# Splitting the first load of a Poisson loss kernel: row 0 of log_input in 16 KB runs, rows 1 to 3 behind it in 48 KB runs

## Chip, cores, metric

One core of one Trainium2 chip. The metric is the device time of one execution in microseconds (us), median over repeated runs; lower is better.

Engines: DVE is VectorE, ACT is ScalarE, SP is the sequencer that issues the loads (SPq in the profile), DMA the core's sixteen transfer engines. x stands for log_input, t for target.

## The reference

```python
batch, dim = 1024, 4096          # log_input and target, float32
loss = np.exp(log_input) - target * log_input
return np.mean(loss, axis=-1)    # 1024 results
```

Two inputs of 16.8 MB are read once, 4 KB are written. Each partition holds 8 neighbouring rows of 4096 elements (16 KB each), so several rows of one partition are one contiguous run in memory.

## The kernel before

All loads are issued by SP on one queue, in this order, each with its own semaphore:

```python
TAIL = [("x", 24), ("t", 12), ("t", 12), ("x", 6), ("t", 5), ("x", 2), ("t", 3)]  # 32nds of row 7
...
    loads = []
    for first, rows in ((0, 4), (4, 2), (6, 1)):
        loads += [("x", first * d, rows * d), ("t", first * d, rows * d)]
    # then TAIL, the pieces of row 7
...
    for i, (what, lo, w) in enumerate(loads):
        if what == "x" and lo in (6 * d, 7 * d):     # rows 6 and 7 reuse the buffer of rows 0 to 3
            free = 1 if lo == 6 * d else 4
            nc.sync.wait_ge(exp_done, free)
            nc.sync.wait_ge(prod_done, free)
        src = x_v if what == "x" else t_v
        dma = nc.sync.dma_start(out=place(what, lo, w), in_=src[:, lo : lo + w])
        dma.then_inc(landed[i] if i < len(loads) - 1 else last_ready, 16)
        if lo < 6 * d:
            early.append(dma.ins)
    before_first_barrier(nc, early)                  # issued ahead of everything else
```

ACT takes exp of one row at a time with the row's sum; DVE multiplies one row of t by the row of x, also with the sum; ACT joins both sums of a row:

```python
    for k, (lo, w, i) in enumerate(x_work):          # ACT, a row at a time
        row, col = lo // d, lo % d
        if col == 0 and row >= 2:
            join(row - 2, k)                         # waits for DVE's product of row - 2
        elif col == 0 and row == 1:
            nc.scalar.wait_ge(exp_done, k)
        nc.scalar.activation(... Exp ...).wait_op(landed[i], 16, "sem-ge")...
        # cut
    for j, (lo, w, i) in enumerate(t_work):          # DVE, a row at a time
        x_load = next(ix for a, wx, ix in x_work if a + wx >= lo + w)
        if j == 0 or x_load > t_work[j - 1][2]:
            nc.vector.wait_ge(landed[x_load], 16)
        nc.vector.tensor_tensor_reduce(... t = t * x, sum ...).wait_op(landed[i], 16, "sem-ge")...
```

The last DVE instruction waits for everything, adds up row 7 and releases the store.

## Time and profile before

| | before |
|---|---|
| time | 84.06 us, 3 runs, 84.04 to 84.06 |
| span of the profiled execution | 82.9 us |
| DVE, ACT busy | 43%, 40% |
| DMA queue | 2016 packets, 95.5% of sixteen engines' time |
| x rows 0 to 3 landed, t rows 0 to 3 landed | 22.10 us, 41.44 us |

The lines of the page and of the timeline are in the prediction below. Two terms it uses: a *packet* is one run of one partition; each of the sixteen engines moves eight partitions of every load, so every load is eight data packets per engine, whatever the length of the runs (the trace has 256 packets of 64 KB for the first two loads). A load has *landed* when the last of the sixteen engines has reported its part.

What ACT and DVE waited for before (columns: total us, times, longest us):

```profile
DVE t_big L175 <- DMA t_big<-in_target_dram: 43.6, 3, 41.4
ACT e_dump L155 <- DMA x_big<-in_log_input_dram: 24.0, 4, 17.8
ACT join_dump L141 <- DVE parts L175: 20.4, 6, 16.3
ACT L155 <- PEq L48: 3.0, 1, 3.0
```

The last line is the wait at the program's first barrier. ACT's two large waits stand one behind the other: 17.8 us for its first row and then 16.3 us for DVE's first product.

### The profile page before, as it was taken

The numbers are of one execution on the slowest core, as the hardware profiler recorded it, in microseconds if no ns is written. First come the engines' busy times: TensorE is split into PE (matmuls) and PEld (weight loads), VectorE is DVE, ScalarE is ACT, GpSimd is POOL, SyncE is SP. The second block draws the span as 40 slices with busy tenths as digits, with TensorE's granted clock in tenths as the row PEclk, the third lists the DMA queues.
The fourth block names the chain that finished last, engine by engine and source line by source line (L and its number), as shares of the span: only waits on it lengthen the run. The fifth ranks groups of instructions, "written<-read, shape, count | busy, mean of one in ns | idle before, by whom it ended". The sixth has DMA issues, their size and how long they took to land.

```text
span 82.9 us, 131 instructions
## 1 busy us (share of the span) xinstructions
DVE 35.6 (43%) x22; ACT 33.2 (40%) x35; POOL 0.3 (0%) x5
## 2 busy tenths in 40 slices
DVE  0000000000000000000099999999469996994992
ACT  0500000000399920000000897979793496019460
POOL 0000000000000000000000000000000000000000
DMA  9199999929999992999699799899899999999950
GB/s 506 63 443 506 506 506 506 443 127 443 506 506 506 506 443 127 443 506 506 269 490 474 316 474 490 380 411 490 364 403 435 443 435 393 433 397 421 393 184 2
DMA packets 2016, 33.56 MB, mean 405 GB/s; under 512 B 352, under 2 KB 608, under 8 KB 1120
## 3 DMA queue, kind: packets, MB, share of 16 engines
q1 hardware_dynamic: 2016, 33.56, 95.5%
HBM read 33.55 MB, written 0.00 MB: 405 GB/s over the span
## 4 chain that ended last, share of the span: by engine, by line
DMA 72%; DVE 18%; issue 4%; SPq 3%; ACT 1%
DMA t_big<-in_target_dram 49%; DMA x_big<-in_log_input_dram 23%; DVE t_big L175 17%; SPq L129 3%; DVE t_big L193 1%; ACT e_dump L155 1%; DVE parts L175 0%; SPq L127 0%; DVE all_loss L193 0%
## 5 line engine op out<-in xcount | busy, mean ns | idle before, releaser
L175 DVE CUSTOM_DVE_ANT_0 t_big<-t_big,x_big 128x4096 f32<-128x4096 f32 (+2 forms) x8 | 26.2, 3306 | 43.8 <-DMA t_big<-in_target_dram 43.6
L155 ACT ACTIVATE e_dump<-x_big 128x4096 f32<-128x4096 f32 (+3 forms) x8 | 21.8, 2730 | 24.2 <-DMA x_big<-in_log_input_dram 24.0
L175 DVE CUSTOM_DVE_ANT_0 t_mid<-t_mid,x_mid 128x4096 f32<-128x4096 f32 x2 | 8.8, 4424 | 2.0 <-DMA t_mid<-in_target_dram 2.0
L141 ACT ACTIVATE join_dump<-parts 128x2 f32<-128x2 f32 x7 | 1.4, 203 | 20.4 <-DVE parts L175 20.4
L155 ACT ACTIVATE e_dump<-x_mid 128x4096 f32<-128x4096 f32 x2 | 7.1, 3568 | 0.0
L155 ACT ACT_TABLE_LOAD x1 | 1.3, 1283 | 3.0 <-PEq L48 3.0
L155 ACT ACTIVATION_READ_ACCUMULATOR e_dump<-x_big 128x1 f32 x8 | 1.5, 186 | 0.0
L141 ACT ACTIVATION_READ_ACCUMULATOR join_dump<-parts 128x1 f32 x7 | 1.3, 186 | 0.0
L193 DVE CUSTOM_DVE_ANT_0 t_big<-t_big,x_big 128x390 f32<-128x390 f32 x1 | 0.6, 566 | 0.1
L175 DVE DVE_READ_ACCUMULATOR2_ANT parts<- 128x1 f32 x7 | 0.6, 81 | 0.0
L155 ACT ACTIVATION_READ_ACCUMULATOR e_dump<-x_mid 128x1 f32 x2 | 0.4, 186 | 0.0
L175 DVE DVE_READ_ACCUMULATOR2_ANT t_big<- 128x1 f32 x3 | 0.2, 83 | 0.0
L136 POOL MEMSET x_big<- 128x6 f32 x1 | 0.1, 103 | 2.5 <-POOLq L48 2.5
L227 POOL MEMSET const-bfloat16-1.0<- 128x1 bf16 x1 | 0.1, 101 | 0.0
L227 POOL MEMSET const-uint8-127<- 128x1 uint8 x1 | 0.1, 101 | 0.0
L227 POOL MEMSET const-float32-0.0<- 128x1 f32 x1 | 0.1, 98 | 0.2 <-issue 0.2
L227 POOL MEMSET const-float32-1.0<- 128x1 f32 x1 | 0.1, 98 | 0.0
L193 DVE DVE_READ_ACCUMULATOR2_ANT all_loss<- 128x1 f32 x1 | 0.1, 84 | 0.0
## 6 DMA issues: line engine op xcount, KB each, us to landing
x_mid<-in_log_input_dram SPq DMA_DIRECT2D x1, 4096.0 KB, 50.2
t_mid<-in_target_dram SPq DMA_DIRECT2D x1, 4096.0 KB, 59.5
x_big<-in_log_input_dram SPq DMA_DIRECT2D x1, 2048.0 KB, 19.8
t_big<-in_target_dram SPq DMA_DIRECT2D x1, 2048.0 KB, 24.3
x_big<-in_log_input_dram SPq DMA_DIRECT2D x1, 1536.0 KB, 15.3
t_big<-in_target_dram SPq DMA_DIRECT2D x2, 768.0 KB, 17.6
x_big<-in_log_input_dram SPq DMA_DIRECT2D x1, 384.0 KB, 18.8
t_big<-in_target_dram SPq DMA_DIRECT2D x1, 320.0 KB, 19.1
```

The costliest lines, as they stand in the source:

```text
L129: dma = nc.sync.dma_start(out=place(what, lo, w), in_=src[:, lo : lo + w])
L136: nc.gpsimd.memset(big["x"][:, 4 * d : 4 * d + n_parts], -1.0).then_inc(ones_done, 1)
L141: nc.scalar.activation(out=join_dump[:, 2 * row : 2 * row + 2], in_=parts[:, 2 * row : 2 * row + 2], func=ACT_F.Copy, scale=inv_d, accum_o ...
L155: nc.scalar.activation(out=e_dump[:, col : col + w], in_=place("x", lo, w), func=ACT_F.Exp, bias=0.0, scale=1.0, accum_out=parts[:, 2 * ro ...
L175: nc.vector.tensor_tensor_reduce(out=place("t", lo, w), in0=place("t", lo, w), in1=place("x", lo, w), scale=-1.0, scalar=0.0, op0=ALU.mult ...
L193: nc.vector.tensor_tensor_reduce(out=place("t", lo, w + n_parts), in0=place("t", lo, w + n_parts), in1=place("x", lo, w + n_parts), scale= ...
L227: nc = _bacc.Bacc("TRN2", target_bir_lowering=False, num_devices=1)
```

## The change

The intent, as far as the diff shows it: let exp of row 0 begin as soon as row 0 is there, instead of when all four rows are. DVE's bookkeeping is changed so that it waits once for each load of x.

```diff
     loads = []
-    for first, rows in ((0, 4), (4, 2), (6, 1)):
+    loads += [("x", 0, d), ("x", d, 3 * d), ("t", 0, 4 * d)]
+    for first, rows in ((4, 2), (6, 1)):
         loads += [("x", first * d, rows * d), ("t", first * d, rows * d)]
...
+    waited = set()
     for j, (lo, w, i) in enumerate(t_work):
...
-        if j == 0 or x_load > t_work[j - 1][2]:
+        if x_load not in waited:
             nc.vector.wait_ge(landed[x_load], 16)
+            waited.add(x_load)
```

## The prediction

> **What bounds the kernel now.** I read the page first. Each compute engine is busy under half of the span, while the DMA row is full almost to the end and the one queue takes 95.5% of the sixteen engines' time:
>
> ```profile
> span 82.9 us, 131 instructions
> DVE 35.6 (43%) x22; ACT 33.2 (40%) x35; POOL 0.3 (0%) x5
> ...
> DVE  0000000000000000000099999999469996994992
> ACT  0500000000399920000000897979793496019460
> ...
> DMA  9199999929999992999699799899899999999950
> ...
> q1 hardware_dynamic: 2016, 33.56, 95.5%
> ...
> DMA 72%; DVE 18%; issue 4%; SPq 3%; ACT 1%
> ```
>
> The two empty-looking slices in the DMA row's first half are not idleness: a 64 KB packet takes 2.418 us and a slice is 2.07 us, so now and then a slice is credited with no finished packet. I checked this in the packet records: chained end to start, the sixteen engines run from 1.0 us to about 80 us with no gap over 0.12 us (the output store apart). The "DVE 18%" of the chain of waits is a detour: from 41.4 to 58.9 us the chain goes through DVE only because the last loads are issued once DVE has freed their buffer, but these loads then wait behind others in the queue. Next, the timeline shows when each load landed (what the idle time in brackets ended on) and when each issue was made:
>
> ```profile
> 0.00 0.38 SPq L129 DMA_DIRECT2D x_big<-in_log_input_dram  x1
> 0.43 0.42 SPq L129 DMA_DIRECT2D t_big<-in_target_dram  x1
> 0.89 0.43 SPq L129 DMA_DIRECT2D x_mid<-in_log_input_dram  x1
> 1.37 0.55 SPq L129 DMA_DIRECT2D t_mid<-in_target_dram  x1
> ...
> 22.10 3.59 ACT L155 ACTIVATE e_dump<-x_big 128x4096 f32<-128x4096 f32 x1 [17.84 <-DMA x_big<-in_log_input_dram]
> ...
> 41.44 4.42 DVE L175 CUSTOM_DVE_ANT_0 t_big<-t_big,x_big 128x4096 f32<-128x4096 f32 x1 [41.44 <-DMA t_big<-in_target_dram]
> ...
> 45.91 0.20 ACT L141 ACTIVATE join_dump<-parts 128x2 f32<-128x2 f32 x1 [16.29 <-DVE parts L175]
> 45.96 0.33 SPq L129 DMA_DIRECT2D x_big<-in_log_input_dram  x1
> ...
> 59.00 0.33 SPq L129 DMA_DIRECT2D x_big<-in_log_input_dram  x1
> ...
> 60.87 4.43 DVE L175 CUSTOM_DVE_ANT_0 t_mid<-t_mid,x_mid 128x4096 f32<-128x4096 f32 x1 [1.96 <-DMA t_mid<-in_target_dram]
> ...
> 70.65 4.42 DVE L175 CUSTOM_DVE_ANT_0 t_big<-t_big,x_big 128x4096 f32<-128x4096 f32 x1 [1.00 <-DMA t_big<-in_target_dram]
> ...
> 80.30 0.39 ACT L155 ACTIVATE e_dump<-x_big 128x256 f32<-128x256 f32 x1 [0.23 <-DMA x_big<-in_log_input_dram]
> ```
>
> To see here: ACT starts at 22.10 when all four rows of log_input (8.4 MB) are there, DVE at 41.44 when four rows of target are. The loads of row 6 are issued at 45.96, when x_mid and t_mid are still in transit (t_mid lands at 60.87), so the queue has about 15 us of work in hand. The last row's loads are issued from 59.00, with everything up to the 70.65 landing still in the queue: some 11.6 us in hand. So no refill ever finds the queue empty. The end is the stream's own end (last log_input piece at 80.28), then one short exp, the last DVE instruction, and the store. The time is therefore: when the stream starts, plus what 33.5 MB take, plus a tail of about 2.6 us that the change does not touch.
>
> **What the Trainium skill says.**
> - "DMA: Bandwidth & Descriptors", section "Where 436 GB/s comes from": 16 ports of 32 bytes at 850 MHz give a ceiling of 435.2 GB/s. The trace agrees: a 64 KB packet in 2.418 us is 27.1 GB/s on an engine, times 16 is 434 GB/s. There is nothing left to win from larger runs.
> - The same page, section "Why small descriptors are slow (HBM only)": each packet carries a fixed overhead of a few cycles. The trace agrees in kind: the records' median packets are 2.418 us (64 KB), 1.213 (32 KB), 0.611 (16 KB). Twice 1.213 less 2.418 is 8 ns per packet, and four times 0.611 less 2.418 over three is 9 ns.
> - The same page, section "Queues, rings and completion order": each engine consumes descriptors in ring order. The trace agrees: the loads land in the order of issue, so a load split in two keeps the place of its bytes in the stream.
> - The same page, "Latency and other measured facts", row "HBM row pitch at large powers of two": copies lose rate at partition pitches of 512 KiB and up. The pitch here is 8 rows of 16 KB, 128 KB, before and after. Row 6 already travels in 16 KB runs at that pitch, at the full 0.611 us (longest 0.636), so this case's trace shows no loss.
>
> **The change part by part.**
> Removed: one issue of 128 runs of 64 KB, that is 8 packets per engine. Added: one issue of 128 x 16 KB, one of 128 x 48 KB, together 16 packets per engine; one more completion write per engine (9 ns in the records); one more issue on SP; one more semaphore wait on DVE. The bytes stay the same.
>
> 1. Stream. From the landings, a row of either input takes (41.44 - 22.10)/4 = 4.835 us in 64 KB runs and (70.65 - 60.87)/2 = 4.89 us in 16 KB runs. The 16 KB row has 8 packets per engine, the 64 KB one 2 per row: 0.055 us for 6 packets, 9 ns each, the same as from the records. Eight more packets per engine are 8 x 9 = 0.07 us, and with the completion write about 0.08 us. All of it is on the path, because the stream has no slack anywhere.
>
> 2. SP. A fifth early issue takes about 0.45 us (the others: 0.38 to 0.55). SP then reaches the first barrier later, and what stands at 2.97 us for ACT (its table load, 1.28 us) moves to about 3.4, done by 4.7. Row 0 arrives later than that (next point), so it is hidden. The first issue is still first, and the second follows while the first has 4.9 us of packets to move, so no engine runs dry: 0.
>
> 3. ACT. Start-up, completion and queueing before the first landing are 22.10 - 4 x 4.835 = 2.76 us. Row 0 lands at 2.76 + 4.89 = 7.65 and exp starts there, 14.45 us earlier; rows 1 to 3 land at about 22.2. Then exp of row 1 runs from 22.2 to 25.9. Exp of row 2 stands behind the join of row 0, which needs DVE's product of row 0, which needs target at 41.5. So ACT stops at 25.9 and not 29.6, and both orders meet again at 45.9. The 14.45 us turn wholly into a longer wait: 0 on the path.
>
> 4. DVE. It begins with target's landing, about 41.52. The new wait between rows 0 and 1 is on data that landed 20 us ago; as an estimate from the 17 ns that the trace gives to SP's own semaphore waits and the 70 ns by which two products overlap now (45.79 against the former's end at 45.86), it costs up to 0.1 us. DVE has 1.96 us of slack before t_mid: 0. The wait that frees the last row's buffer moves from 58.94 to about 59.1, against 11.6 us of queue in hand: 0.
>
> Sum: 84.06 + 0.08 + 0 + 0 + 0 = 84.14 us, say 84.1.
>
> **The rivals.**
> - The earlier exp shortens the program (the change's likely intent). For it: ACT idles 17.84 us and begins 14 us earlier after the change. Against it: ACT's next wait is 16.29 us for DVE's product, and DVE waits 41.44 us for target, which comes behind all of log_input's four rows still. For a gain, target's bytes would have to move forward; they don't. This rival would give some 80 us or less; I give it 1 in 100.
> - The start of the stream changes. The first packet of each engine took 2.76 to 3.63 us against 2.418 later, so 0.3 to 1.2 us go there, and the engine with 3.63 keeps some 0.3 us of lag to the end of the early loads, where it sets the landings. If the excess is one latency per engine, short first packets pay it just the same and nothing moves. If short packets even out the laggard, up to 0.3 us are won (83.8); if each of the first few short packets pays some of it, 0.3 to 0.5 us are lost (84.5). This, and not the packet overhead, sets the width of my range.
> - Shorter runs lower the rate of HBM, or the queue holds too few entries. For it: twice the packets. Against it: row 6's 16 KB packets at full rate, and up to ten loads in the queue after 59.00 with issues of 0.33 to 0.45 us each, none held up. A loss of 5% on the first 8.4 MB would be 1 us (85.1); 2% of the whole time would need 1.7 us.
>
> **Range and chances.** The centre is 84.1. The runs before differ by 0.02 us, so the width comes from the start of the stream: minus 0.3 to plus 0.5 us, hence 83.8 to 84.6. The limits of 2% lie at 82.4 and 85.7, both far outside: faster 0.01, within 2% 0.975, slower 0.015.
>
> **What would show it.** Step 1: target's first landing at 41.4 to 41.7, and the queue's 2016 packets grown by 128 data packets and 16 completions, 2160; the DMA row full as now. Step 2: ACT's table load near 3.4. Step 3: exp of row 0 at about 7.65, of row 1 at about 22.2, then ACT idle for some 20 us until the join at about 46. Step 4: products of rows 0 to 3 from about 41.5 to 59, then still idle nearly 2 us before t_mid; the last log_input piece at 80.3 to 80.4. I would be wrong if the first row landed much later than 8 us, if rows 1 to 3 did not land by 22.5, or if a gap opened in the stream.

## The result

83.97 us, median of 6 runs (83.87 to 84.15), against 84.05 us (84.01 to 84.12) for the kernel before beside it. The ratio is 0.9991, 95% interval 0.9979 to 1.0004: the same within 2%.

The page of the changed kernel:

```profile
span 82.8 us, 133 instructions
...
ACT  0323930000394000000000897979793496019360
...
DMA  5999999888999991999599699899899999999950
...
q1 hardware_dynamic: 2160, 33.56, 95.5%
```

The ACT row now has a first block near the left edge, exp of row 0, and a hole behind it. From the 23rd slice on it is the row of before but for one digit. The queue has its 2160 packets and the same share.

The timeline of the changed kernel:

```profile
3.48 1.28 ACT L157 ACT_TABLE_LOAD   x1 [3.48 <-PEq L49]
7.46 3.59 ACT L157 ACTIVATE e_dump<-x_big 128x4096 f32<-128x4096 f32 x1 [2.71 <-DMA x_big<-in_log_input_dram]
...
21.97 3.59 ACT L157 ACTIVATE e_dump<-x_big 128x4096 f32<-128x4096 f32 x1 [10.80 <-DMA x_big<-in_log_input_dram]
...
41.33 4.42 DVE L179 CUSTOM_DVE_ANT_0 t_big<-t_big,x_big 128x4096 f32<-128x4096 f32 x1 [41.33 <-DMA t_big<-in_target_dram]
...
45.80 0.20 ACT L143 ACTIVATE join_dump<-parts 128x2 f32<-128x2 f32 x1 [20.12 <-DVE parts L179]
...
60.75 4.42 DVE L179 CUSTOM_DVE_ANT_0 t_mid<-t_mid,x_mid 128x4096 f32<-128x4096 f32 x1 [1.95 <-DMA t_mid<-in_target_dram]
...
70.55 4.43 DVE L179 CUSTOM_DVE_ANT_0 t_big<-t_big,x_big 128x4096 f32<-128x4096 f32 x1 [1.02 <-DMA t_big<-in_target_dram]
...
80.22 0.39 ACT L157 ACTIVATE e_dump<-x_big 128x256 f32<-128x256 f32 x1 [0.30 <-DMA x_big<-in_log_input_dram]
```

Exp of row 0 begins 14.64 us earlier (7.46 against 22.10). The join of row 0, which stands behind it on ACT, begins 0.11 us earlier. All later landings move by 0.08 to 0.14 us, the last one by 0.08 us: one shift, made before 41 us and carried to the end.

Its waits:

```profile
ACT join_dump L143 <- DVE parts L179: 24.2, 6, 20.1
ACT e_dump L157 <- DMA x_big<-in_log_input_dram: 19.7, 5, 10.8
ACT L157 <- PEq L49: 3.5, 1, 3.5
```

19.7 + 24.2 + 3.5 = 47.4 us, against 24.0 + 20.4 + 3.0 = 47.4 us before. ACT's gain has turned into waiting, to the tenth of a microsecond.

What is left is the small shift, and its sign: I had forecast 0.08 us more, the two traces show about 0.1 us less. Each is a single execution (84.23 us before, 84.15 us after, both slower than the other executions in the two first sets), and four traces of the kernel before will differ by as much (t complete at 41.26 to 41.42 us). The experiments had to tell whether this was scatter or something real, and to check the two statements it rests on: only the stream of transfers counts, and a packet costs 8 to 9 ns.

### The profile page after: what moved, and what is told of

It is laid out like the page before. It is cut to its first block, busy times and chain, and to the rows that moved or that the text cites. A ratio compares the mean times of both kernels' runs of the same rounds, so it can differ in the third digit from the quotient of the medians.

```text
span 82.8 us, 133 instructions
## 1 busy us (share of the span) xinstructions
DVE 35.6 (43%) x22; ACT 33.2 (40%) x35; POOL 0.3 (0%) x5
## 2 busy tenths in 40 slices
DMA packets 2160, 33.56 MB, mean 405 GB/s; under 512 B 368, under 2 KB 624, under 8 KB 1136
## 3 DMA queue, kind: packets, MB, share of 16 engines
q1 hardware_dynamic: 2160, 33.56, 95.5%
## 4 chain that ended last, share of the span: by engine, by line
DMA 72%; DVE 13%; issue 10%; SPq 3%; ACT 1%
DMA t_big<-in_target_dram 49%; DMA x_big<-in_log_input_dram 23%; DVE t_big L179 12%; SPq L131 3%; DVE t_big L197 1%; ACT e_dump L157 1%; DVE parts L179 0%; SPq L129 0%; DVE all_loss L197 0%
## 5 line engine op out<-in xcount | busy, mean ns | idle before, releaser
L157 ACT ACTIVATE e_dump<-x_big 128x4096 f32<-128x4096 f32 (+3 forms) x8 | 21.8, 2730 | 19.8 <-DMA x_big<-in_log_input_dram 19.7
L143 ACT ACTIVATE join_dump<-parts 128x2 f32<-128x2 f32 x7 | 1.4, 203 | 24.2 <-DVE parts L179 24.2
```

Of the source, the lines that this page charges most:

```text
L143: nc.scalar.activation(out=join_dump[:, 2 * row : 2 * row + 2], in_=parts[:, 2 * row : 2 * row + 2], func=ACT_F.Copy, scale=inv_d, accum_o ...
L157: nc.scalar.activation(out=e_dump[:, col : col + w], in_=place("x", lo, w), func=ACT_F.Exp, bias=0.0, scale=1.0, accum_out=parts[:, 2 * ro ...
```

## The experiments

Twelve runs were made, four on one chip at a time with the kernel before beside them (below in this order: the first four, the next four and the four repeats each shared a chip). All were correct. For the start of the stream I read two things in the trace that the page doesn't show. First, the packet records: end of each engine's first packet, less the packet's steady duration (2.418, 1.815 or 0.611 us for 64, 48 or 16 KB), which I call the engine's start. Second, the time at which each engine reported its part of t's rows 0 to 3 (in the run with t split, rows 1 to 3), first and last of sixteen.

| kernel, first packet | starts: fastest, median, slowest | t landed: first to last engine |
|---|---|---|
| before, 64 KB | 1.53, 1.92, 2.41 | 40.60 to 41.42 |
| before_again, 64 KB | 1.59, 1.86, 2.30 | 40.61 to 41.29 |
| before_third, 64 KB | 1.58, 1.90, 2.27 | 40.62 to 41.26 |
| before_fourth, 64 KB | 1.54, 1.83, 2.36 | 40.62 to 41.37 |
| long_first, 48 KB | 1.69, 1.98, 2.18 | 40.80 to 41.29 |
| long_first_two, 48 KB | 1.63, 1.94, 2.17 | 40.76 to 41.25 |
| changed kernel, 16 KB | 1.65, 1.83, 2.22 | 40.76 to 41.31 |
| after_again, 16 KB | 1.46, 1.81, 2.04 | 40.79 to 41.14 |
| after_third, 16 KB | 1.39, 1.75, 2.02 | 40.70 to 41.17 |
| exp_late, 16 KB | 1.29, 1.76, 1.92 | 40.67 to 41.00 |
| target_early, 16 KB | 1.21, 1.82, 2.05 | 40.76 to 41.23 |
| four_16k, 16 KB | 1.48, 1.81, 2.00 | 40.85 to 41.31 |
| first_4k, 4 KB | not clear | 40.59 to 41.28 |
| sixteen_4k, 4 KB | not clear | 41.73 to 42.23 |

(With 4 KB packets the first sixteen records need not be the sixteen engines' first packets, so no start is given.)

The fastest starts with 16 KB are not kept. Each engine can be followed by chaining a record to the one that ends where it begins. After its first 128 KB the slowest engine of every run with a start in the table still stands where it is given there, within 0.03 us, but the fastest then stands at 1.64, 1.69 and 1.58 us in the three traces of the changed kernel, against 1.53 to 1.59 before. In after_again, for example, the engine that was first sat idle for 0.22 us after its first packet.

**after_again.** The changed kernel, unedited, in more rounds.

> The changed kernel again, in more rounds, to learn whether its 0.08 us are real. Theory 'start evens out' (short first packets bring the sixteen engines closer together, worth about -0.16 us, packet overhead +0.08 us): 83.97 us, ratio to before 0.998 to 0.9995. Rival 'packet overhead alone': 84.13 us, ratio 1.001. Rival 'nothing but scatter': a ratio on either side of 1 with an interval that holds it.

Measured: 83.95 us (83.89 to 84.05), before 84.13 (84.00 to 84.40, 11 runs), ratio 0.9978, interval 0.9964 to 0.9993. A small gain that here is clear of scatter; packet overhead alone does not describe it. (The ratio lies just under the 0.998 of the theory.) The kernel before scatters more than the changed one in these rounds.

**long_first.** Same split, order turned round.

```diff
-    loads += [("x", 0, d), ("x", d, 3 * d), ("t", 0, 4 * d)]
+    loads += [("x", 0, 3 * d), ("x", 3 * d, d), ("t", 0, 4 * d)]
```

> The same split with the order turned round: rows 0 to 2 first in 48 KB runs, row 3 behind in 16 KB runs. Same packets, bytes and waits. Theory 'start evens out': the first packet is long again, so the laggard of 0.3 us comes back and only the overhead stays: 84.13 us, ratio 1.001, the landings of one load spread over about 0.8 us as before. Rival 'the split as such helps': 83.97 us as the changed kernel.

Measured: 84.09 us (84.02 to 84.33), ratio 0.9998, interval 0.9981 to 1.0015. The time favours the theory, but the lower end of its interval lies at the rival's ratio. One detail of mine missed: the landings of t spread over 0.49 us and not 0.8, for the slowest engine started at 2.18, between the two groups.

**exp_late.** The changed loads, ACT held back.

```diff
+        if k == 0:
+            nc.scalar.wait_ge(landed[1], 16)
         nc.scalar.activation(            # exp of row 0
```

> The changed loads, but the exp of row 0 also waits for rows 1 to 3, so that ACT begins at about 22 us as before. Theory 'the early exp is off the path': as the changed kernel within 0.1 us, 83.97 us. Rival 'the early exp is what saves the 0.08 us': 84.05 to 84.15 us.

Measured: 83.95 us (83.84 to 84.23), ratio 0.9984, interval 0.9966 to 1.0002. As the changed kernel (83.95 us on the same chip, after_again). The timeline shows more delay on ACT than I had asked for, because the table load moved behind the new wait as well:

```profile
21.72 1.28 ACT L159 ACT_TABLE_LOAD   x1 [21.72 <-DMA x_big<-in_log_input_dram]
23.02 3.59 ACT L159 ACTIVATE e_dump<-x_big 128x4096 f32<-128x4096 f32 x1
...
41.03 4.42 DVE L181 CUSTOM_DVE_ANT_0 t_big<-t_big,x_big 128x4096 f32<-128x4096 f32 x1 [41.03 <-DMA t_big<-in_target_dram]
```

ACT begins at 23.02, later even than before, and the time stays. The early exp contributes nothing that can be seen; whatever the change wins, it wins in the stream.

**target_early.** t split in the same way, and row 0 of t brought forward, so that DVE begins early too.

```diff
-    loads += [("x", 0, d), ("x", d, 3 * d), ("t", 0, 4 * d)]
+    loads += [("x", 0, d), ("t", 0, d), ("x", d, 3 * d), ("t", d, 3 * d)]
```

> Row 0 of log_input, row 0 of target, then rows 1 to 3 of each: now DVE too can begin, at about 12.3 us instead of 41.4. Theory 'the stream alone sets the end': 8 more packets per engine and a completion write, +0.08 us on the changed kernel, 84.05 us, although both engines begin 14 and 29 us earlier than before; row 6's loads are issued near 17 us and wait in the queue. Rival 'the late start of DVE costs': 82.4 us or less (2% and more).

Measured: 84.04 us (83.98 to 84.10), ratio 0.9988, interval 0.9973 to 1.0002; expected 84.05. Its timeline:

```profile
12.19 4.43 DVE L179 CUSTOM_DVE_ANT_0 t_big<-t_big,x_big 128x4096 f32<-128x4096 f32 x1 [12.19 <-DMA t_big<-in_target_dram]
...
16.71 0.33 SPq L131 DMA_DIRECT2D x_big<-in_log_input_dram  x1
...
41.25 4.43 DVE L179 CUSTOM_DVE_ANT_0 t_big<-t_big,x_big 128x4096 f32<-128x4096 f32 x1 [24.63 <-DMA t_big<-in_target_dram]
...
80.15 0.39 ACT L157 ACTIVATE e_dump<-x_big 128x256 f32<-128x256 f32 x1 [0.27 <-DMA x_big<-in_log_input_dram]
```

DVE begins 29 us earlier, and row 6's first load is issued at 16.71 and not at 45.96. The last piece of x lands when it always did. This is the strongest test of the first statement: earlier compute and earlier issues are worth nothing while the queue never runs dry.

**before_again.** The kernel before against itself.

> The kernel before against itself, with a second trace: ratio 1.000 within 0.0015; shows how large a ratio scatter alone gives, and whether the laggard engine and the 0.8 us spread of one load's landings are there in another execution. If the spread is then 0.55 us as in the changed kernel's trace, the theory of the evened-out start has no ground.

Measured: 84.09 us (83.94 to 84.48), before beside it 83.97 (83.92 to 84.61), ratio 1.0007, interval 0.9976 to 1.0039. On this chip single runs of one and the same kernel scatter by up to 0.7 us, so no time of this call can settle 0.1 us. The trace says more: slowest start 2.30, spread of the landings 0.68 us (0.82 in the first trace). That lies between the 0.8 and the 0.55 of the expectation, and settles nothing yet.

**four_16k.** Rows 0 to 3 of x as four loads of 16 KB runs.

```diff
-    loads += [("x", 0, d), ("x", d, 3 * d), ("t", 0, 4 * d)]
+    loads += [("x", k * d, d) for k in range(4)] + [("t", 0, 4 * d)]
```

> Rows 0 to 3 of log_input as four loads in 16 KB runs, 32 packets per engine. With 8.5 ns a packet and 9 ns a completion: 24 packets and 3 completions more than before, +0.23 us. Packet overhead alone: 84.28 us. With the evened-out start (-0.16 us): 84.12 us. Rival 'shorter runs lower HBM's rate': over 84.6 us.

Measured: 84.18 us (84.06 to 84.42), ratio 1.0015, interval 0.9989 to 1.0042: by the scatter alone inconclusive between 84.12 and 84.28. HBM's rate does not fall, since that would have given over 84.6. The table is sharper: the *first* engine to finish t does so at 40.85, 0.24 us later than the mean 40.61 of the kernel before (expected overhead 0.23), while the *last* one does so at 41.31, slightly earlier than the mean 41.34 of before.

**sixteen_4k.** The kernel before, its first load cut into sixteen loads of 4 KB runs. They share one semaphore and the engines wait for the full count of 256, so that the waits of ACT and DVE stay those of before (the counts in the waits are edited to match).

```diff
-        dma = nc.sync.dma_start(out=place(what, lo, w), in_=src[:, lo : lo + w])
...
+        for c in cuts.get(i, [w]):       # cuts = {0: [1024] * 16}
+            dma = nc.sync.dma_start(out=place(what, a, c), in_=src[:, a : a + c])
...
```

> The kernel before with its first load cut into sixteen loads of 4 KB runs on one semaphore: the waits of the engines stay as before, 128 packets per engine instead of 8. Theory of 8.5 ns per packet on the path: 120 x 8.5 ns + 15 x 9 ns = +1.15 us, less up to 0.16 us for the start: 85.0 to 85.2 us. Rival 'packet overhead is hidden in the queue': 83.9 to 84.1 us.

Measured: 85.06 us (85.05 to 85.09), ratio 1.0119, interval 1.0094 to 1.0144. As expected, and the rival is out. The first engine finishes t at 41.73, 1.12 us later than before's mean. Less fifteen completion writes of 9 ns that is 0.98 us for 120 packets, 8.2 ns a packet. The figure depends on the engine chosen (the last one is 0.89 us later than before's mean, 42.23 against 41.34), but the records agree with it: sixteen 4 KB packets last 16 x 0.159 = 2.544 us, the 64 KB packet 2.418, so 8.4 ns for each of fifteen packets more. Its page and timeline:

```profile
DMA packets 4176, 33.56 MB, mean 401 GB/s; under 512 B 592, under 2 KB 848, under 8 KB 3408
...
q1 hardware_dynamic: 4176, 33.56, 96.2%
...
0.00 8.19 SPq L133 DMA_DIRECT2D x_big<-in_log_input_dram  x16
...
8.71 2.97 SPq L133 DMA_DIRECT2D x_mid<-in_log_input_dram  x1
11.72 1.08 SPq L133 DMA_DIRECT2D t_mid<-in_target_dram  x1
```

The share of the queue *rose* (96.2 from 95.5%) while the kernel became slower: per-packet overhead counts as busy time, so a full queue is no proof of an efficient one.

**first_4k.** The same edit with the first load cut in two, 4 KB and 60 KB runs.

```diff
+    cuts = {0: [1024, 15 * 1024]}
```

> The kernel before with its first load cut in two, 4 KB runs and then 60 KB runs, on one semaphore; the waits of the engines stay as before (exp begins at about 22 us). As many packets as the changed kernel. Theory 'start evens out': what matters is that the first packet is short, so 83.9 to 84.0 us. Rival 'packet overhead alone': 84.13 us.

Measured: 84.02 us (83.89 to 84.09), ratio 0.9993, interval 0.9967 to 1.0018: inconclusive in time. The trace is against a simple form of my theory: the landings spread over 0.69 us, as with 64 KB runs. One short first packet is not enough. Nor did the 60 KB packets bring the lag: their first records begin between 2.74 and 3.46 us, so 0.72 us of spread stood already when the eight 4 KB packets were over. In sixteen_4k the same eight packets were reported between 3.20 and 3.70 us (here between 3.08 and 3.82), and t there spreads over 0.50 us. Two equal first loads with two spreads: either what is queued behind them matters, or chance alone is of this size. Neither is tested.

**before_third, before_fourth, after_third, long_first_two.** Unedited repeats, to see whether the difference of the starts holds.

> The kernel before once more, for a third trace of its start. So far the slowest engine ended its first packet 2.41 and 2.30 us later than a packet at the steady rate issued at time 0 would (0.14 and 0.30 us behind the second slowest), and the last of target's first landing came at 41.42 and 41.29. Theory 'long first packets leave a slower laggard': 2.25 us or more here, landing at 41.25 or later. Rival 'chance': a value between 1.9 and 2.2 as with 16 KB runs first.

> The changed kernel once more, for a further trace of its start. So far, with 16 KB runs first: slowest engine 2.22, 2.04, 1.92 (exp_late), 2.05 (target_early) and 2.00 us (four_16k). Theory: 2.2 us or less, target's first landing complete by 41.3, time 0.05 to 0.2 us under the kernel before. Rival 'chance': as before, 2.25 us or more.

> A fourth trace of the kernel before, the same expectation as the third: theory 2.25 us or more for the slowest engine's start, rival 'chance' 1.9 to 2.2 us.

> The order turned round (48 KB runs first), a second trace. In its first trace the slowest engine stood at 2.18 us, between the two groups, and its time was 0.9998 of before. Theory: start 2.15 to 2.4 us and a time equal to before or up to 0.1 us over it (overhead paid, no gain). Rival 'the split as such helps': start under 2.1 us and a time 0.1 us or more under before.

Measured, with before beside them at 84.00 us (83.93 to 84.11, 9 runs): before_third 84.00 us (83.91 to 84.08), ratio 0.9998 (0.9985 to 1.0010), slowest start 2.27; before_fourth 84.16 us (83.99 to 84.32), ratio 1.0013 (0.9999 to 1.0028), slowest start 2.36; after_third 84.00 us (83.90 to 84.10), ratio 0.9998 (0.9984 to 1.0011), slowest start 2.02; long_first_two 84.06 us (84.02 to 84.08), ratio 1.0004 (0.9991 to 1.0016), slowest start 2.17. All four starts came out as the theory has it. The time of after_third did not: no gain of 0.05 us or more was seen on this chip. (The expectation of before_third has two distances in the wrong order: the slowest engine was 0.30 us behind the second slowest in the first trace and 0.14 us in before_again.)

The three traces of the changed kernel beside the four of before: the slowest start is 2.09 us on average against 2.34, 0.24 us better before rounding, and the groups don't overlap. With 0.08 us of overhead to pay back, 0.16 us should remain. t lands complete at 41.21 against 41.34 on average, 0.13 us earlier. The average engine gains nothing: the mean of the sixteen reports of t is 40.93 us against 40.91. The change brings the engines closer together, the first later and the last earlier. The order turned round does part of the same (slowest start 2.17 and 2.18), and the first trace of the changed kernel (2.22) lies above it, so 48 KB and 16 KB in front are not told apart. The three sets of timed runs give ratios of 0.9991, 0.9978 and 0.9998, which is 0.08, 0.18 and 0.02 us less. So: the start of the slowest engine is shown to be better in the changed kernel than before; a gain in time of about 0.1 us is plausible, clear of scatter in one set of three.

No version beats both kernels clearly. The lowest medians are those of the changed loads (after_again and exp_late, both 83.95 us), and their difference from before is of the size of the scatter between chips.

## Why the prediction was right or wrong

The forecast "the same, 83.8 to 84.6 us" held, and for its reason: the stream sets the time, and the early exp is off its path. The number itself was a mild test, since the range of 0.8 us is ten times the change that was forecast. Two dates of "What would show it" were sharper, and both came too early: t complete at 41.31 us, not 41.4 to 41.7, and the last piece of x at 80.20 us, not 80.3 to 80.4. No gap opened in the stream (0.12 us at most, as before, when the records are chained in the same way). By its steps:

1. **Stream.** The size of the overhead was right, and so was that it is on the path: 8.2 ns a packet and 1.12 us in the exaggerated case, 0.24 us with 24 packets more. (Both delays are the first engine's; the whole kernel lost 1.00 us in sixteen_4k, 1.19% of 84.06.) For the changed kernel itself the first engine finishes t at 40.75 us on average (three traces) against 40.61, 0.14 us later where I had said 0.08; the fastest engine's later start, 1.64 us on average against 1.56 when followed through 128 KB, covers the rest. That the stream has "no slack anywhere" was too strong: the engines are not equally late, and only the slowest sets a landing.
2. **SP.** Right: the table load moved to 3.48 (said: 3.4), was done by 4.76, and exp began at 7.46.
3. **ACT.** Right: 7.46 (said 7.65) and 21.97 (said about 22.2), then a wait of 20.12 us. Both dates came early, as a better start would have it, which I had not put into the sum. exp_late and target_early show that the zero on the path is a zero.
4. **DVE.** Right, even cautious: the new wait cost nothing to be seen. The products of rows 0 and 1 lie 4.35 us apart before and after (41.44 and 45.79; 41.33 and 45.68).

Two readings of the page and the queue were loose, without harm to the sum: three slices of the DMA row's first half look empty and not two (the page counts a packet in the slice in which it begins), and the "ten loads in the queue" are nine with the one being issued, for t_mid had landed by then.

**The step that failed** is the sum, which left out the start of the stream and so, as far as so small a number can be told, got its sign wrong: 84.14 forecast, 83.97 measured. (The forecast ratio of 1.001 lies outside two of the three intervals; only one of the three excludes 1.) The prediction named the missing term in its second rival ("If short packets even out the laggard, up to 0.3 us are won (83.8)") and put it into the range but not into the centre. Measured over the traces, that term is -0.24 us, against +0.08 for the packets. My support for leaving it at zero, "one latency per engine, short first packets pay it just the same", is what the repeats contradict: the slowest start falls from 2.27 to 2.41 us with 64 KB packets, through 2.17 and 2.18 with 48 KB, to 1.92 to 2.22 with 16 KB. The laggard's delay does stay to the end, as said: in the first trace the last sixteen reports of x still spread over 0.81 us (79.47 to 80.28), as t's had at 41 us.

Of the rivals, "the earlier exp shortens the program" and "shorter runs lower the rate" are both refuted; too few entries in the queue did not matter here either, for the changed kernel's issues took 0.33 to 0.52 us each. What stays open is why the slowest engine is further behind with 64 KB runs in front. That it is the length of its first packet is not shown: in before_fourth the slowest engine's first packet begins only at 2.36 us and then takes the steady 2.42 us, so its whole delay stood before that packet. The packet records name no engine, so I can't say whether it is always the same one, and first_4k shows that the length of the very first packet is not the whole of it.

## What to carry to other kernels

When one queue is full from the first microsecond to the last, and stays so when issues move, ask of a change only what it does to the bytes, the packets and the two ends of the stream; an engine that starts 14 or 29 us earlier merely waits elsewhere. A split of a load costs its packets (here 8 x 8 to 9 ns per engine and load), which is cheap, so split where it releases something and not where the next wait stands right behind. And look at the landing of the slowest engine and not at the average: the slowest one's lag of a few tenths from its first packet was carried through the whole run here.

## What the Trainium skill lacked or had wrong

- "DMA: Bandwidth & Descriptors", section "Why small descriptors are slow (HBM only)": it gives a fixed overhead of about 3 cycles per packet for the engine's internal bus, and besides it 32 bytes of descriptor metadata for each operation. At the 850 MHz and 32 bytes a cycle that the same page states for a port, the two would be 4.7 ns (an estimate). The runs show 8 to 9 ns per packet in the records, and 8.2 ns in the landings of sixteen_4k. What the rest is, no run here shows.
- The same page, section "Latency and other measured facts": it gives a single figure for the first byte (about 600 ns), which fits the first packet's record (begun at 1.0 us, 0.6 us after the first issue's end at 0.38), and nothing on how unevenly sixteen engines start on this path (its one row on slower engines is about the loads that GpSimd issues). Counted from the beginning of the span, the runs with first packets of 16 to 64 KB show a start of 1.5 to 1.7 us for the fastest engine, after its first 128 KB, and 1.9 to 2.4 us for the slowest, whose lag is kept for 80 us.
- Among the pages on DMA that I read, none says how many loads SP can have in the queue before an issue is held up. In sixteen_4k the eighteenth issue, at 8.71 us, took 2.97 us instead of 0.43 us. By the engines' reports four of the seventeen loads before it had landed, so thirteen were outstanding. But their number alone does not decide: the issue before it, at 8.24 us, took 0.43 us behind twelve, while in target_early the last load's issue, at 57.26 us, took 0.95 us behind nine, and none of these landed meanwhile. The kernel before never issues behind more than eight, and none of its issues was held up. What sets the limit, no run here shows.
